# A mixer kernel: background steps drawn twice per merge-gate chunk, transposes of p in steps of their own, the last RG-LRU inputs cut earlier, copies of q and k ahead of their squares

## The chip, the cores and the metric

The kernel runs on one core of one Trainium2 chip. The metric is the device time of one execution in microseconds (us). A core has TensorE (PE, matmuls and transposes), VectorE (DVE), ScalarE (ACT), GpSimd (POOL) and SyncE (SP, which here issues the loads of weights). Each takes its own instructions in the order written for it and waits on semaphores for the others.

## What is computed

One layer of an encoder on 512 tokens of width 1024, in float32:

```python
x = x + FFN_RES * _swiglu(_rmsnorm(x, norm_ffn1[l]), w_ffn1_gu[l], w_ffn1_down[l])
...
h = _rmsnorm(x, norm_mix[l])
xr, gr, q, k, v, ga, gb = jnp.split(h @ w_in[l], splits, axis=-1)
xc = _centred_dwconv(xr, conv_w[l], conv_b[l]).astype(jnp.float32)
...
y_lru = ((h_fwd + h_bwd) * jax.nn.gelu(gr.astype(jnp.float32))).astype(x.dtype)
...
y_att = _neighbourhood_attention(q, k, v, rel_pos_bias[l]).astype(x.dtype)
y = jax.nn.sigmoid(ga) * y_lru + jax.nn.sigmoid(gb) * y_att
x = x + y @ w_out[l]
x = x + FFN_RES * _swiglu(_rmsnorm(x, norm_ffn2[l]), w_ffn2_gu[l], w_ffn2_down[l])
```

`h_fwd` and `h_bwd` are the recurrence `_rglru_scan` over `xc` forward and backward. It needs two sigmoid gates (a block-diagonal product with `xc`), an exponential, a square root and a scan over the tokens, in each direction. The attention has 16 heads of width 64; a query sees a window of 8 rows by 16 columns of the 8 x 64 token grid, with a learned bias and a softmax; `q` and `k` are normalized per head.

## The kernel before

**Precision and dense work.** A float32 product is made of three matmuls of a rounded high part and a low part: `wh` by `xh`, `wh` by `xl`, `wl` by `xh`. Weights come in chunks of 128 x 1024 values (512 KB) by a DMA of SP into `wraw` (three buffers); ACT (line 138), or DVE for every second chunk of the merge gates (line 140), casts to `wh`, and DVE subtracts to get `wl` (line 141), four buffers each. I call the matmuls that work on such chunks *dense*; they read 512 columns and fill an accumulator in PSUM.

**PSUM.** Two pools of four banks: `acc` for dense products (and for the second half of the scores in the second half of the heads), `aux` for everything else on PE: gate products of the RG-LRU, transposes, scores, PV.

**Stages.** First feed-forward; then the mixer; then the second feed-forward. The mixer's dense work, in its order:
- eight chunks for `xr` (`feat_chunk`, lines 165 to 167), each followed by the convolution;
- token groups (`tok_group`, lines 761 to 763) for q, k and v of the first eight heads (hf = 0), then of the other eight (hf = 1): four chunks each, 96 dense matmuls, into all four `acc` banks. The evictions at a group's end free the banks for the next group: the copies of q and k on ACT (line 774, each followed by a square at line 775), those of v on DVE (line 785);
- merge gates (`gates`, line 947): 24 chunks of 24 dense matmuls, eight for the GeLU gate, eight for each merge gate; each chunk is evicted on DVE to a `pair` tile (line 953);
- eight chunks of the output projection.

**Background.** Two generators hold the other work: lane "lru" (`lru`, line 642) and lane "att" (`heads`, line 806). `weave(rate)` is called after each chunk and draws from each lane as many steps as the table `RATE` gives for the phase ("xr", "t0" for the first half's q, k, v, "t1" for the second's, "g" for the gates); what a step issues then stands in the program behind that chunk. So the tables `LRU_PLAN` (which step of lane "lru" does what) and `RATE` (how many steps per chunk) set the order on all engines, apart from instructions marked `high_priority`, which a scheduler puts ahead of others on their engine where their inputs allow.

**Lane "lru".** For each of eight feature blocks f: `fetch` loads the gate weights; `cut` splits the convolved block into `ch` (ACT, line 138) and `cl` (DVE, line 141); `gates` does 12 groups of matmuls (line 675) and four sigmoids on ACT (line 685), and its next block waits for them; then `use`, `decay` (an exponential, line 705), `root` (a square root, line 710) and `scan` (DVE, lines 717 and 719, and an add at 720). Activations of a kind are kept together by `act`, since each change of kind needs a table load on ACT.

**Lane "att".** For each pair of heads fi of a half: `start` transposes q and k (lines 828 and 830) into two `aux` banks, which ACT and DVE empty into `qh`, `ql` (line 835), `kh`, `kl` (line 837); `scores` (line 854) makes the products, DVE adds the bias and takes the maximum (line 866, output `so` and `nmx`), ACT takes the exponential (869), DVE scales (875); `turn` transposes p (line 883) into an `aux` bank, copied to `PT` by ACT (886); `apply` multiplies with v (line 895, PV), copied to `att` by ACT (905). In the first half a unit is half a pair's keys (`n2` = 0 or 1), in the second a whole pair. One step holds the scores of unit i, PV of unit i - 2, the transposes of q and k for the next pair and the turns of unit i - 1; in the second half a yield lies between the turns of n2 = 0 and n2 = 1.

Of the kernel before, what the change touches and what calls it, by code (L numbers as in the profile page):

```python
# [11 lines left out]
AF = mybir.ActivationFunctionType  # L12
# [7 lines left out]
KT = D // P  # L20
# [37 lines left out]

LRU_PLAN = [
    ("root", range(4), range(39, 47)),  # L60
    ("scan", range(4), range(41, 49)),
    ("cut", range(8), (0, 3, 8, 13, 18, 23, 44, 48)),
    ("fetch", range(8), (0, 4, 9, 14, 19, 24, 44, 48)),
    ("gates", range(8), (2, 7, 12, 17, 22, 27, 47, 51)),
    ("decay", range(4), range(29, 37)),
# [8 lines left out]
]  # L74

RATE = {
    "xr": {"lru": 2.5, "att": 0.0},
    "t0": {"lru": 3, "att": 0.0},
    "t1": {"lru": 2, "att": 0.75},
    "g": {"lru": 3, "att": 0.85},  # L80
}


# [1 line left out]
def block_kernel(ctx: ExitStack, tc, a, out):  # L85
    nc = tc.nc
# [20 lines left out]
    def big_t(dt=F32, shape=(P, T), n="b"):  # L107
        return big.tile(list(shape), dt, tag="big", bufs=NBIG, name=nm(n))
# [55 lines left out]
    def mm3(ps, wh, wl, xh, xl, first, last, skip=False):  # L164
        nc.tensor.matmul(ps, wh, xh, start=first, stop=False, skip_group_check=skip)  # L165
        nc.tensor.matmul(ps, wh, xl, start=False, stop=False, skip_group_check=skip)  # L166
        mark["mm"] = nc.tensor.matmul(ps, wl, xh, start=False, stop=last, skip_group_check=skip)  # L167

    def feat_chunk(src, nk, xh, xl, ps, k0, ktot, act=True):
        H, L = load_w(src, nk * P, act)  # L170
        for k in range(nk):
            s = slice(k * P, (k + 1) * P)
            kk = k0 + k
            mm3(ps, H[:, s], L[:, s], xh[kk], xl[kk], kk == 0, kk == ktot - 1)


    def make_xg(gcol, tag):
# [350 lines left out]
    xh, xl, ssum, one, square = make_xg(C_G1, "a")  # L528
# [53 lines left out]
    xh, xl, ssum = nxt["v"][:3]  # L582
# [154 lines left out]
    for f in range(KT):  # L737
        ps = acc_t()
# [13 lines left out]
    def tok_group(w, hf):  # L752
        pss = [acc_t() for _ in range(NCB)]
        for kp in range(4):
            H, L = load_w(a["wqkv"][w * 2 + hf, kp], 1024)
            for j in range(NCB):
                tj = slice(j * P, (j + 1) * P)
                for k in range(2):
                    kk = kp * 2 + k
                    s = slice(k * T, (k + 1) * T)  # L760
                    nc.tensor.matmul(pss[j], xh[kk][:, tj], H[:, s], start=kk == 0, stop=False)  # L761
                    nc.tensor.matmul(pss[j], xl[kk][:, tj], H[:, s], start=False, stop=False)  # L762
                    mark["mm"] = nc.tensor.matmul(pss[j], xh[kk][:, tj], L[:, s], start=False, stop=kk == KT - 1)  # L763
            if kp < 3:
                weave(RATE[phase[0]])
        return pss

    def qk_raw(w, hf, st):
        raws = []
        for j, ps in enumerate(tok_group(w, hf)):  # L770
            t = big_t(n="qk")
            sq = big_t(n="sq")
            with tc.high_priority():
                nc.scalar.activation(t, ps, AF.Copy)
            nc.scalar.activation(sq, t, AF.Square)
            nc.vector.reduce_sum(st[:, w, j, :], sq.rearrange("p (h d) -> p h d", d=HD), axis=AX.X)
            raws.append(t)
        weave(RATE[phase[0]])
        return raws

# [25 lines left out]
    def heads(hf, raws, st):  # L806
# [9 lines left out]
        for w in range(2):  # L816
            for j in range(NCB):
                t = raws[w][j].rearrange("p (h d) -> p h d", d=HD)
# [95 lines left out]
        LB, LC = ATT_LAG[hf]  # L914
        for i in range(len(units) + LC):
            if i < len(units):
                fi, n2s = units[i]
                last = scores(fi, n2s)
                if i >= LC and 1 in units[i - LC][1]:
                    apply(units[i - LC][0], last)  # L920
                if 0 in n2s:
                    if fi < 3:
                        start(fi + 1)
                    if hf * 4 + fi + 1 < KT:
                        bias(hf * 4 + fi + 1)
            for n2 in (0, 1):
                if 0 <= i - LB < len(units) and n2 in units[i - LB][1]:
                    for hp in range(2):
                        turn(units[i - LB][0], n2, hp)
                if hf == 1 and n2 == 0:  # L930
                    yield
            if len(units) <= i < len(units) + LC and 1 in units[i - LC][1]:
                apply(units[i - LC][0])
            yield

    att = [None] * KT
# [10 lines left out]
    def gates(w, fs, fn, scale=1.0):  # L947
        q = [pair_t() for _ in range((len(fs) + 1) // 2)]
        for i, f in enumerate(fs):
            ps = acc_t()  # L950
            feat_chunk(a["wg3"][w * KT + f], KT, xh, xl, ps, 0, KT, f % 2 == 0)
            with tc.high_priority():
                nc.vector.tensor_tensor(q[i // 2][:, i % 2], ps, rb, ALU.mult)
            weave(RATE[phase[0]])
        for i, t in enumerate(q):
            n = min(2, len(fs) - 2 * i)
            nc.scalar.activation(t[:, :n], t[:, :n], fn, scale=scale)
        return [(f, q[i // 2][:, i % 2]) for i, f in enumerate(fs)]
# [126 lines left out]
```

## Time and profile before

| | |
|---|---|
| median of 3 runs | 1127.6 us (1127.58 to 1127.77) |
| the profiled execution | 1127.92 us |
| its span in the trace | 1125.7 us |
| busy: PE, DVE, ACT, POOL | 99%, 74%, 53%, 5% |
| mean granted clock of PE | 1.0 |

The span is the time from the first to the last instruction of the profiled execution; 2.2 us of its time lie outside it. A row of a timeline gives the start in us from the span's beginning, the duration, the engine, the line, the operation, the tiles it writes and reads, the shape, a count, and in brackets the idle time ahead of it with who ended it. Matmuls are pipelined: a row's duration is longer than the distance to the next start, and the distance is what counts. A list of waits adds up the idle time of an engine by the line that waited and the instruction that released it.

### The profile page before, as it was taken

How to read it: one execution, taken by the hardware profiler on the slowest of the kernel's cores; microseconds unless marked ns; L12 is line 12 of the kernel's file. 1: busy time of each engine (PE TensorE's matmuls, PEld its weight loads, DVE VectorE, ACT ScalarE, POOL GpSimd, SP SyncE). 2: the span in 40 equal slices, each digit the busy share in tenths (PEclk: the TensorE clock that was granted, in tenths of full speed). 3: DMA queues.
4: the chain of work that ended last, by engine and by line, in shares of the span. 5: the costliest groups of instructions: out<-in, count | busy, mean ns of one | idle time of the engine just before them, and what ended most of it. 6: DMA issues, size and time to landing. Idle time of an engine off the chain costs nothing.

```text
span 1125.7 us, 17414 instructions
## 1 busy us (share of the span) xinstructions
PE 1114.5 (99%) x6867; PEld 983.4 (87%) x6867; DVE 834.9 (74%) x1294; ACT 592.9 (53%) x897; POOL 52.3 (5%) x116
## 2 busy tenths in 40 slices
PE   9999999999999999999999999999999999999998
PEld 8899999988888777777888888888999999998887
DVE  7888888893736865899655877659688888894552
ACT  8554554563533668687464445446445445464330
POOL 0000000000000341120110000000000000000000
PEclk9999999999999999999999999999999999999999
DMA  7242333443423686573443342355134233252421
GB/s 265 93 127 80 114 112 95 132 134 98 143 80 103 164 231 174 151 193 94 135 147 103 94 124 64 105 180 183 57 95 118 90 112 114 94 169 94 131 75 38
DMA packets 46770, 138.04 MB, mean 123 GB/s; under 512 B 7008, under 2 KB 10592, under 8 KB 46688
## 3 DMA queue, kind: packets, MB, share of 16 engines
q1 hardware_dynamic: 39744, 118.31, 33.8%
q0 software_dynamic: 6368, 18.36, 5.9%
q8 instruction: 54, 0.88, 0.3%
q10 hardware_dynamic: 576, 0.26, 0.1%
q14 instruction: 28, 0.23, 0.1%
HBM read 120.12 MB, written 8.39 MB: 114 GB/s over the span
## 4 chain that ended last, share of the span: by engine, by line
PE 96%; DVE 2%; issue 1%; ACT 1%; DVEq 0%; ACTq 0%
PE acc L289 29%; PE acc L165 11%; PE acc L166 11%; PE acc L167 11%; PE aux L289 5%; PE aux L167 4%; PE aux L165 4%; PE aux L166 4%; PE acc L761 3%; PE acc L763 3%; PE acc L762 3%; PE aux L883 1%; PE aux L895 1%; PE aux L675 1%; PE aux L854 1%
## 5 line engine op out<-in xcount | busy, mean ns | idle before, releaser
L138 ACT ACTIVATE wh<-wraw 128x1024 fp32r<-128x1024 f32 (+3 forms) x242 | 239.8, 993 | 327.5 <-PE acc L289 95.9
L141 DVE TENSOR_TENSOR wl<-wraw,wh 128x1024 fp32r<-128x1024 f32 (+3 forms) x254 | 289.5, 1142 | 143.4 <-ACT wh L138 140.1
L289 PE MATMUL acc<-s,wh 128*128 128x256 f32 x1216 | 220.5, 283 | 0.0
L289 PEld LDWEIGHTS acc<-s,wh 128*128 128x128 f32 x1216 | 189.7, 192 | 0.0
L289 PE MATMUL acc<-s,wl 128*128 128x256 f32 x608 | 172.1, 283 | 0.0
L165 PE MATMUL acc<-xh,wh 128*128 128x512 f32 x304 | 120.4, 396 | 0.0
L167 PE MATMUL acc<-xh,wl 128*128 128x512 f32 x304 | 118.9, 391 | 0.0
L166 PE MATMUL acc<-xl,wh 128*128 128x512 f32 x304 | 118.8, 391 | 0.0
L289 PEld LDWEIGHTS acc<-s,wl 128*128 128x128 f32 x608 | 116.8, 192 | 0.0
L289 PE MATMUL acc<-xh,wl 128*128 128x256 f32 x304 | 86.0, 283 | 0.0
L289 PE MATMUL acc<-xl,wh 128*128 128x256 f32 x304 | 86.0, 283 | 0.0
L289 PE MATMUL acc<-xh,wh 128*128 128x256 f32 x304 | 86.0, 283 | 0.0
L761 PE MATMUL acc<-wh,xh 128*128 128x512 f32 x192 | 75.8, 396 | 1.9 <-DVE v L785 1.4
L762 PE MATMUL acc<-wh,xl 128*128 128x512 f32 x192 | 75.1, 391 | 0.0
L763 PE MATMUL acc<-wl,xh 128*128 128x512 f32 x192 | 75.0, 391 | 0.0
L323 DVE TENSOR_TENSOR wraw<-wraw,pair 128x1024 f32<-128x1024 f32 x57 | 69.5, 1220 | 0.8
L165 PE MATMUL aux<-hh,wh 128*128 128x512 f32 (+1 forms) x181 | 69.9, 386 | 0.0
L166 PE MATMUL aux<-hl,wh 128*128 128x512 f32 (+1 forms) x181 | 69.9, 386 | 0.0
L167 PE MATMUL aux<-hh,wl 128*128 128x512 f32 (+1 forms) x181 | 69.9, 386 | 0.0
L167 PE MATMUL acc<-hh,wl 128*128 128x512 f32 (+1 forms) x176 | 67.9, 386 | 0.0
L166 PE MATMUL acc<-hl,wh 128*128 128x512 f32 (+1 forms) x176 | 67.9, 386 | 0.0
L165 PE MATMUL acc<-hh,wh 128*128 128x512 f32 (+1 forms) x176 | 67.9, 386 | 0.0
(212 smaller groups left out, 2206.8 us busy)
## 6 DMA issues: line engine op xcount, KB each, us to landing
wraw<-wqkv SPq DMA_DIRECT2D x24, 512.0 KB, 4.5
wraw<-wg SPq DMA_DIRECT2D x24, 512.0 KB, 3.6
wraw<-w1d SPq DMA_DIRECT2D x22, 512.0 KB, 3.6
wraw<-w2d SPq DMA_DIRECT2D x22, 512.0 KB, 3.6
pair<-w2s SPq DMA_DIRECT2D x20, 512.0 KB, 3.6
wraw<-w2s SPq DMA_DIRECT2D x20, 512.0 KB, 3.6
wraw<-w1s SPq DMA_DIRECT2D x18, 512.0 KB, 3.6
pair<-w1s SPq DMA_DIRECT2D x18, 512.0 KB, 3.7
```

Of the source, the lines that this page charges most:

```text
L138: nc.scalar.activation(H, raw, AF.Copy)
L141: nc.vector.tensor_tensor(L, raw, H.bitcast(F32), ALU.subtract)
L165: nc.tensor.matmul(ps, wh, xh, start=first, stop=False, skip_group_check=skip)
L166: nc.tensor.matmul(ps, wh, xl, start=False, stop=False, skip_group_check=skip)
L167: mark["mm"] = nc.tensor.matmul(ps, wl, xh, start=False, stop=last, skip_group_check=skip)
L289: nc.tensor.matmul(o, w_[:, c], x_, start=first and m + k == 0 and w_ is H and x_ is xh_, stop=m + k == 4 and w_ is L, skip_group_check=True)
L323: nc.vector.tensor_tensor(t, t, o, ALU.add)
L675: prev, mm = mm, nc.tensor.matmul(ps[d][b], W[w][o, c], X[x][o], start=x == 1, stop=w + x == 0)
L761: nc.tensor.matmul(pss[j], xh[kk][:, tj], H[:, s], start=kk == 0, stop=False)
L762: nc.tensor.matmul(pss[j], xl[kk][:, tj], H[:, s], start=False, stop=False)
L763: mark["mm"] = nc.tensor.matmul(pss[j], xh[kk][:, tj], L[:, s], start=False, stop=kk == KT - 1)
L854: mm = hold(nc.tensor.matmul(ps[hp][:, i * 256 : (i + 1) * 256], q_[o, n * P : (n + 1) * P], keys(k_[o]), start=k_ is kl, stop=q_ is ql))
```

## The change

Five edits, in two tables and three functions:

- `LRU_PLAN`: the last two cuts (f = 6 and 7) move from steps 44 and 48 to steps 41 and 45; the scans of f = 0 to 3 move from steps 41..48 to 42, 43, 44, 46..50.
- `RATE`: lane "lru" runs at 2.75 instead of 2.5 steps per chunk in "xr" and 3.25 instead of 3 in "t0". In the gates the rates become 1.5 and 0.7, and `feat_chunk` draws once in the middle of each chunk as well as `gates` at its end, so 3 and 1.4 steps per chunk where they were 3 and 0.85.
- `qk_raw`: all four copies of a group are issued first, then the four squares, each behind the last copy.
- `heads`: in the gates a yield lies between a unit's scores and the turns of the unit before, and the turns of n2 = 0 and of n2 = 1 are steps of their own in both halves.
- `gates` passes the rate to `feat_chunk` for the draw in the middle.

```diff
--- before.py
+++ after.py
@@ -58,8 +58,8 @@
 
 LRU_PLAN = [
...
-    ("scan", range(4), range(41, 49)),
-    ("cut", range(8), (0, 3, 8, 13, 18, 23, 44, 48)),
+    ("scan", range(4), (42, 43, 44, 46, 47, 48, 49, 50)),
+    ("cut", range(8), (0, 3, 8, 13, 18, 23, 41, 45)),
...
@@ -74,10 +74,10 @@
 ]
 
 RATE = {
-    "xr": {"lru": 2.5, "att": 0.0},
-    "t0": {"lru": 3, "att": 0.0},
+    "xr": {"lru": 2.75, "att": 0.0},
+    "t0": {"lru": 3.25, "att": 0.0},
...
-    "g": {"lru": 3, "att": 0.85},
+    "g": {"lru": 1.5, "att": 0.7},
 }
 
 
@@ -166,12 +166,14 @@
         nc.tensor.matmul(ps, wh, xl, start=False, stop=False, skip_group_check=skip)
         mark["mm"] = nc.tensor.matmul(ps, wl, xh, start=False, stop=last, skip_group_check=skip)
 
-    def feat_chunk(src, nk, xh, xl, ps, k0, ktot, act=True):
+    def feat_chunk(src, nk, xh, xl, ps, k0, ktot, act=True, mid=None):
         H, L = load_w(src, nk * P, act)
         for k in range(nk):
             s = slice(k * P, (k + 1) * P)
             kk = k0 + k
             mm3(ps, H[:, s], L[:, s], xh[kk], xl[kk], kk == 0, kk == ktot - 1)
+            if mid is not None and k == nk // 2 - 1:
+                weave(mid)
 
 
     def make_xg(gcol, tag):
@@ -767,14 +769,15 @@
 
     def qk_raw(w, hf, st):
         raws = []
-        for j, ps in enumerate(tok_group(w, hf)):
+        for ps in tok_group(w, hf):
             t = big_t(n="qk")
+            with tc.high_priority():
+                copy = nc.scalar.activation(t, ps, AF.Copy)
+            raws.append(t)
+        for j, t in enumerate(raws):
             sq = big_t(n="sq")
-            with tc.high_priority():
-                nc.scalar.activation(t, ps, AF.Copy)
-            nc.scalar.activation(sq, t, AF.Square)
+            after(nc.scalar.activation(sq, t, AF.Square), copy)
             nc.vector.reduce_sum(st[:, w, j, :], sq.rearrange("p (h d) -> p h d", d=HD), axis=AX.X)
-            raws.append(t)
         weave(RATE[phase[0]])
         return raws
 
@@ -923,12 +926,14 @@
                         start(fi + 1)
                     if hf * 4 + fi + 1 < KT:
                         bias(hf * 4 + fi + 1)
-            for n2 in (0, 1):
-                if 0 <= i - LB < len(units) and n2 in units[i - LB][1]:
+            if phase[0] == "g":
+                yield
+            if 0 <= i - LB < len(units):
+                for k, n2 in enumerate(units[i - LB][1]):
+                    if k:
+                        yield
                     for hp in range(2):
                         turn(units[i - LB][0], n2, hp)
-                if hf == 1 and n2 == 0:
-                    yield
             if len(units) <= i < len(units) + LC and 1 in units[i - LC][1]:
                 apply(units[i - LC][0])
             yield
@@ -948,7 +953,7 @@
         q = [pair_t() for _ in range((len(fs) + 1) // 2)]
         for i, f in enumerate(fs):
             ps = acc_t()
-            feat_chunk(a["wg3"][w * KT + f], KT, xh, xl, ps, 0, KT, f % 2 == 0)
+            feat_chunk(a["wg3"][w * KT + f], KT, xh, xl, ps, 0, KT, f % 2 == 0, RATE[phase[0]])
             with tc.high_priority():
                 nc.vector.tensor_tensor(q[i // 2][:, i % 2], ps, rb, ALU.mult)
             weave(RATE[phase[0]])
```

PE, DVE and ACT have the same number of instructions before and after, and POOL and SP the same DMAs. Where they stand is shown at three places.

DVE from the last scans to the eviction of v of the first half (`wl` are low parts of weights; `cl` is the low part of block 7, the last one cut, which the last gate products wait for; `th<-gate,gate` are scans, `v<-acc` the evictions). Before:

```order
L720 TENSOR_TENSOR th_730_4291<-th_730_4291,th_736_4328 128x512
L717 SCALAR_TENSOR_TENSOR th_753_4401<-gate_698_4186,gate_699_4187 128x512
L719 SCALAR_TENSOR_TENSOR th_754_4404<-gate_701_4195,gate_702_4196 128x512
L141 TENSOR_TENSOR wl_854_4901<-wraw_852_4899,wh_853_4900 128x1024
L720 TENSOR_TENSOR th_753_4401<-th_753_4401,th_754_4404 128x512
L141 TENSOR_TENSOR wl_857_4939<-wraw_855_4937,wh_856_4938 128x1024
L141 TENSOR_TENSOR cl_820_4765<-xc_692_4162,ch_819_4764 128x512
L141 TENSOR_TENSOR wl_863_4989<-wraw_861_4987,wh_862_4988 128x1024
L785 TENSOR_SCALAR v_840_4870<-acc_794_4642,rcol_594_3718 128x512
L785 TENSOR_SCALAR v_841_4872<-acc_795_4643,rcol_594_3718 128x512
L785 TENSOR_SCALAR v_842_4874<-acc_796_4644,rcol_594_3718 128x512
L785 TENSOR_SCALAR v_843_4876<-acc_797_4645,rcol_594_3718 128x512
```

and after, from the cut of block 7 on, whose `cl` is the second row:

```order
L713 TENSOR_TENSOR gate_693_4147<-gate_693_4147,th_750_4371 128x512
L141 TENSOR_TENSOR cl_800_4657<-xc_706_4206,ch_799_4656 128x512
L713 TENSOR_TENSOR gate_696_4156<-gate_696_4156,th_754_4404 128x512
L722 TENSOR_TENSOR th_697_4162<-th_697_4162,th_700_4169 128x512
L719 SCALAR_TENSOR_TENSOR th_730_4291<-gate_663_4016,gate_664_4017 128x512
L721 SCALAR_TENSOR_TENSOR th_733_4298<-gate_666_4025,gate_667_4026 128x512
L141 TENSOR_TENSOR wl_839_4852<-wraw_837_4850,wh_838_4851 128x1024
L722 TENSOR_TENSOR th_730_4291<-th_730_4291,th_733_4298 128x512
L719 SCALAR_TENSOR_TENSOR th_750_4371<-gate_692_4146,gate_693_4147 128x512
L721 SCALAR_TENSOR_TENSOR th_754_4404<-gate_695_4155,gate_696_4156 128x512
L722 TENSOR_TENSOR th_750_4371<-th_750_4371,th_754_4404 128x512
L141 TENSOR_TENSOR wl_856_4921<-wraw_854_4919,wh_855_4920 128x1024
```

The last cl stood behind the scans and two wl; it now stands ahead of two pairs of scans and their adds, and the evictions of v begin behind five more rows, with no cl among them.

ACT at the end of the group for k of the second half (`qh`, `kh` are the high parts of one pair of heads, `qk<-acc` the copies that free the accumulators, `sq` the squares, `wh` a cast of weights). Before:

```order
L834 ACTIVATE qh_907_5260<-aux_905_5250,gq8_3677 128x4x128
L138 ACTIVATE wh_985_5606<-wraw_984_5605 128x1024
L836 ACTIVATE kh_909_5262<-aux_906_5251,small_78 128x512
L774 ACTIVATE qk_916_5302<-acc_877_5088 128x512
L775 ACTIVATE sq_917_5303<-qk_916_5302 128x512
L774 ACTIVATE qk_918_5307<-acc_878_5089 128x512
L775 ACTIVATE sq_919_5308<-qk_918_5307 128x512
L774 ACTIVATE qk_920_5312<-acc_879_5090 128x512
L775 ACTIVATE sq_921_5313<-qk_920_5312 128x512
L774 ACTIVATE qk_922_5317<-acc_880_5091 128x512
L775 ACTIVATE sq_923_5318<-qk_922_5317 128x512
```

and after:

```order
L837 ACTIVATE qh_907_5263<-aux_905_5253,gq8_3677 128x4x128
L839 ACTIVATE kh_909_5265<-aux_906_5254,small_78 128x512
L775 ACTIVATE qk_916_5305<-acc_877_5101 128x512
L775 ACTIVATE qk_917_5307<-acc_878_5102 128x512
L138 ACTIVATE wh_985_5606<-wraw_984_5605 128x1024
L775 ACTIVATE qk_918_5309<-acc_879_5103 128x512
L775 ACTIVATE qk_919_5311<-acc_880_5104 128x512
L779 ACTIVATE sq_920_5313<-qk_916_5305 128x512
L779 ACTIVATE sq_921_5316<-qk_917_5307 128x512
L779 ACTIVATE sq_922_5319<-qk_918_5309 128x512
L779 ACTIVATE sq_923_5322<-qk_919_5311 128x512
```

The cast of weights stood ahead of kh and of all copies and now stands behind kh and two copies; the squares, which alternated with the copies, follow all four.

PE in the merge gates around the transposes of p (`ident,p`) of one pair of heads (`ident,qk` are the transposes of the next pair's q and k, `acc<-xh,wh` and its like dense matmuls). Before, behind the third scores of the second half and a PV:

```order
L830 MATMUL aux_1235_6866<-ident_83,qk_916_5302 128x8x16
L830 MATMUL aux_1235_6866<-ident_83,qk_918_5307 128x8x16
L830 MATMUL aux_1235_6866<-ident_83,qk_920_5312 128x8x16
L830 MATMUL aux_1235_6866<-ident_83,qk_922_5317 128x8x16
L883 MATMUL aux_1242_6887<-ident_83,p_1177_6615 128x128 x4
L165 MATMUL acc_1246_6901<-xh_482_3088,wh_1248_6903 128x512
L166 MATMUL acc_1246_6901<-xl_483_3089,wh_1248_6903 128x512
L883 MATMUL aux_1244_6894<-ident_83,p_1180_6625 128x128 x4
L167 MATMUL acc_1246_6901<-xh_482_3088,wl_1249_6904 128x512
```

and after:

```order
L165 MATMUL acc_1232_6815<-xh_488_3094,wh_1234_6817 128x512
L166 MATMUL acc_1232_6815<-xl_489_3095,wh_1234_6817 128x512
L167 MATMUL acc_1232_6815<-xh_488_3094,wl_1235_6818 128x512
L886 MATMUL aux_1236_6834<-ident_83,p_1169_6538 128x128 x4
L886 MATMUL aux_1238_6841<-ident_83,p_1172_6548 128x128 x4
L165 MATMUL acc_1232_6815<-xh_490_3096,wh_1234_6817 128x512
L166 MATMUL acc_1232_6815<-xl_491_3097,wh_1234_6817 128x512
L167 MATMUL acc_1232_6815<-xh_490_3096,wl_1235_6818 128x512
```

The eight transposes of p stood behind the transposes of q and k, four and four with two dense matmuls between them; they now stand in the middle of a chunk, with dense matmuls on both sides, half a chunk or more behind the scores.

## The prediction

> **What bounds the kernel now.** I read the page's busy times first, then the list of TensorE's (PE's) waits, then the timeline of PE, VectorE (DVE) and ScalarE (ACT) around each wait. The page's first line and the whole list of waits (engine, line waited at, who released it; total us, times, longest):
>
> ```profile
> PE 1114.5 (99%) x6867; PEld 983.4 (87%) x6867; DVE 834.9 (74%) x1294; ACT 592.9 (53%) x897; POOL 52.3 (5%) x116
> PE aux L675 <- DVE cl L141: 1.4, 2, 1.2
> PE acc L761 <- DVE v L785: 1.4, 1, 1.4
> PE aux L883 <- ACT att L905: 1.2, 1, 1.2
> PE aux L131 <- DVE pol L600: 1.1, 1, 1.1
> PE aux L289 <- ACT wh L138: 0.9, 1, 0.9
> PE aux L883 <- DVE nmx L866: 0.7, 2, 0.4
> PE aux L883 <- DVE kl L837: 0.6, 1, 0.6
> PE acc L761 <- ACT qk L774: 0.5, 1, 0.5
> ```
>
> PE is busy for 99% of the span, so the time is PE's work plus these waits, 7.8 us in all. The change moves instructions and removes none (the order holds 6615 rows on PE before and after, and as many on DVE and ACT), so PE's work stays and only waits can come or go. Two rows lie in stages that the change doesn't touch: pol (1.1) at the start and wh at L289 (0.9) in the first feed-forward. That leaves 5.8 us that the change can reach, in the token groups and the merge gates, plus what a wait costs beyond its idle time. Two of the waits on PE (start, duration, line, idle before):
>
> ```profile
> 473.28 0.39 PE L761 MATMUL acc<-wh,xh 128*128 128x512 f32 x1
> 474.87 0.50 PE L675 MATMUL aux<-cl,wh 64*128 64x512 f32 x2 [1.20 <-DVE cl L141]
> ...
> 478.65 0.39 PE L762 MATMUL acc<-wh,xl 128*128 128x512 f32 x1
> 478.88 0.39 PE L763 MATMUL acc<-wl,xh 128*128 128x512 f32 x1
> 480.64 0.50 PE L761 MATMUL acc<-wh,xh 128*128 128x512 f32 x1 [1.38 <-DVE v L785]
> ```
>
> A dense matmul follows the last by 0.23 us (478.65 to 478.88). Over the first wait the starts lie 1.59 apart: 0.23 is due, 1.20 is idle, 0.16 is refilling the pipeline. Over the second: 1.76 - 0.23 - 1.38 = 0.15. So each wait costs its idle time and 0.16.
>
> **The change part by part.** *The cut of the last gate blocks earlier (plan steps 41 and 45 for 44 and 48), scans later.* Why PE waited at 474.87 and 480.64, on DVE and on ACT:
>
> ```profile
> 473.00 1.22 DVE L141 TENSOR_TENSOR wl<-wraw,wh 128x1024 fp32r<-128x1024 f32 x1
> 474.13 0.68 DVE L141 TENSOR_TENSOR cl<-xc,ch 128x512 fp32r<-128x512 f32 x1
> 478.70 1.23 DVE L141 TENSOR_TENSOR wl<-wraw,wh 128x1024 fp32r<-128x1024 f32 x1 [3.89 <-ACT wh L138]
> 479.85 2.71 DVE L785 TENSOR_SCALAR v<-acc,rcol 128x512 f32<-128x512 f32 x4
> ```
>
> ```profile
> 475.88 1.84 ACT L685 ACTIVATE pair<-aux,small 128x512 f32<-128x512 f32 x3 [3.76 <-PE aux L675]
> 477.61 1.07 ACT L138 ACTIVATE wh<-wraw 128x1024 fp32r<-128x1024 f32 x1
> ...
> 479.27 1.28 ACT L705 ACT_TABLE_LOAD   x1
> 480.56 0.72 ACT L705 ACTIVATE gate<-gate,sn 128x512 f32<-128x512 f32 x1
> ```
>
> The last cl stood behind the scans and a weight's wl, and landed 0.06 us before PE started at 474.87. The late gate block made the sigmoids late (475.88), these the weight cast (477.61), this the wl (478.70), and behind it on DVE stood the eviction of v that frees PE's accumulator. So it is one lateness, paid twice. After the change both cl stand ahead of the scans they stood behind, and the last gate block lies 48 dense matmuls ahead of the end of the v group, where it lay 11 ahead. Both cl waits (1.4) go. The v wait goes if the longer chain fits: how long the sigmoids of the gate block before took after its last matmul, on PE and on ACT:
>
> ```profile
> 464.65 0.39 PE L675 MATMUL aux<-ch,wh 64*128 64x512 f32 x2
> ```
>
> ```profile
> 466.91 1.83 ACT L685 ACTIVATE pair<-aux,small 128x512 f32<-128x512 f32 x3
> ```
>
> The sigmoids ended at 468.74, 3.7 us after the block's end at 465.04. Behind them ACT now has a table load (1.29 to the next start), three exponentials (3 x 0.72) and a weight cast (1.07), then DVE a wl (1.15 to the next start) and the eviction (0.79 from its start at 479.85 to PE's at 480.64): 3.7 + 1.3 + 2.2 + 1.1 + 1.15 + 0.8 = 10.2 us, against 48 x 0.23 = 11.0. It fits by 0.8 us, so I count the 1.4 as gone, and keep 1.4 for the range.
>
> In this trace a table load holds ACT for 1.28 us and the next activation starts 1.29 after it. The Trainium skill ("ScalarE: Activation LUTs", section What ACT_TABLE_LOAD costs) adds a drain of about 1.38 us to every switch. By that price the chain would be about 11.6 us and 0.6 us of the v wait would stay; the rows at 479.27 and 480.56 leave no room for such a drain, so I don't take it.
>
> *Copies of q and k first; scans ahead of ql and kl.* The next token-group end, DVE and then ACT:
>
> ```profile
> 527.03 0.75 DVE L835 SCALAR_TENSOR_TENSOR ql<-aux,gq,qh 128x512 fp32r<-128x512 f32 x1
> 527.69 1.22 DVE L717 TENSOR_TENSOR_SCAN th<-gate,gate 128x512 f32<-128x512 f32 x1
> 528.82 1.20 DVE L141 TENSOR_TENSOR wl<-wraw,wh 128x1024 fp32r<-128x1024 f32 x1
> 529.94 0.75 DVE L837 SCALAR_TENSOR_TENSOR kl<-aux,small,kh 128x512 fp32r<-128x512 f32 x1
> ```
>
> ```profile
> 528.86 0.59 ACT L774 ACTIVATE qk<-acc 128x512 f32<-128x512 f32 x1
> ```
>
> PE waited for the first copy (0.5; it frees an accumulator) and for kl (0.6; it frees the aux buffer of the second transposes of p). A cast of weights stood ahead of the copy on ACT, a scan and a wl ahead of kl on DVE. In the changed order kh and two copies come ahead of that cast, and kl stands directly behind ql: both waits go, 1.1. The squares are later by at most three copies (under 2 us), and nothing on PE reads them before the next heads. The price: the scans now stand ahead of the first head's ql and kl, for which the first scores wait, and these now come 24 dense matmuls behind their transposes instead of 28. This place is tight by my reading; I take nothing for it, and one scan and a wl (1.2 + 1.2 less the cover) gives at most 1 us for the range.
>
> *Transposes of p in steps of their own.* PE and ACT at the two waits in the merge gates:
>
> ```profile
> 660.91 0.38 PE L854 MATMUL aux<-kl,qh 64*128 64x256 f32 x2
> ...
> 663.05 0.60 PE L830 MATMUL aux<-ident,qk 128*128 128x128 f32 x4
> 663.90 0.66 PE L883 MATMUL aux<-ident,p 128*128 128x128 f32 x4 [0.25 <-DVE nmx L866]
> ...
> 682.13 0.40 PE L166 MATMUL acc<-xl,wh 128*128 128x512 f32 x1
> 683.75 0.66 PE L883 MATMUL aux<-ident,p 128*128 128x128 f32 x4 [1.22 <-ACT att L905]
> ```
>
> ```profile
> 683.12 0.57 ACT L905 ACTIVATE att<-aux 128x512 f32<-128x512 f32 x1
> ```
>
> In both, transposes of p ask for an aux buffer directly behind scores, PV or the transposes of q and k, which hold the four there are. In the changed order no transposes of p in the gates stand behind scores: at least 12 dense matmuls (2.8 us) lie between. The att copy that came 1.2 late has then the time it needs, and nmx too: 1.2 + 0.3 (0.7 in the list less the 0.4 below) go. The other nmx wait, at the transposes behind the second q and k of the first half, keeps its place in both orders: 0.4 stays. The same matmuls stand in about as many pieces between dense ones, so PE gains or loses nothing by the cutting itself.
>
> *What is new at the end.* The last PV moves from the last gates chunk's end to two and a half chunks earlier; it had covered PE while the last chunk was evicted and combined. DVE there:
>
> ```profile
> 732.40 0.69 DVE L953 TENSOR_TENSOR pair<-acc,rstd 128x512 f32<-128x512 f32 x1 [2.17 <-PE acc L167]
> ...
> 734.93 0.69 DVE L975 SCALAR_TENSOR_TENSOR pair<-pair,att 128x512 f32<-128x512 f32 x1 [0.45 <-ACT att L905]
> ...
> 737.11 0.69 DVE L141 TENSOR_TENSOR yl<-pair,yh 128x512 fp32r<-128x512 f32 x1 [0.76 <-ACT yh L138]
> ```
>
> The chain ends at 737.80; without the wait for att (0.45) at 737.35, 4.95 us after the eviction's start. PE comes to that yl after 22 dense matmuls of the output projection, 22 x 0.23 = 5.06. It just fits; I take 0.1 us, 0.5 for the range.
>
> **Sum.** Gone: 1.4 + 1.4 + 0.5 + 0.6 + 1.2 + 0.3 = 5.4 us idle in seven waits, and 7 x 0.16 = 1.1 of refilling: 6.5. New: 0.1. The profiled execution took 1127.9 us (span 1125.7 and 2.2 around it), so 1121.5; against the median of 1127.6, which is 0.3 less, 1121.2.
>
> **The rivals.**
> 1. *The lateness of the LRU lane only shifts (0.17).* DVE and ACT do the same work; if the v eviction stays late (1.4 + 0.16) and kl at the first scores costs some 0.5, 2.1 us come back: 1123.3. For it: the fits of 0.8 and less. Against: at 480 us DVE had idled 3.89 before the wl, so it has room.
> 2. *The aux buffers only change hands in the merge gates (0.12).* Score steps come 36 and 48 dense matmuls apart instead of 72 and 48; the 1.5 there and its refilling (0.3) come back at other instructions: 1123.0. Both rivals together: 1125.1.
> 3. *Slower: DVE falls behind in the gates (0.04).* One score step on DVE, first and last rows:
>
> ```profile
> 663.07 0.42 DVE L866 CUSTOM_DVE_ANT_0 so<-aux,bm 128x256 f32<-128x256 f32 x1
> ...
> 669.43 0.61 DVE L875 TENSOR_SCALAR p<-p,rs 128x256 f32<-128x256 f32 x2
> ```
>
> That is 7.0 us, and a gates chunk needs about 2.6 more (eviction 0.69, wl 1.22, one combine 0.69). Between the first two score steps, 36 matmuls apart, PE takes 36 x 0.23 + 2.7 (660.91 to 663.65) = 11.0 us, and DVE needs 7.0 + 1.5 x 2.6 = 10.9: full. Scores hold two of four accumulators; if a chunk's eviction comes to stand behind a whole softmax, PE waits from the point at which that is later than the next chunk's 5.5 us: 7.0 - 5.5 = 1.5 a chunk. At both chunks of all four steps that is 12 us: 1133. Against: the steps after the second are 48 apart with 16 transposes and a PV besides, and the evictions have priority.
> 4. *It does not do what it says (0.08).* Each wait is replaced by one of the same size, because what is late is the weights' arrival: 1127.6. Against: no row of PE's list names a DMA.
>
> **How the numbers follow.** My forecast has 0.59, at 1121.2. The low end is all reachable waits gone with the 0.4 that I left and a larger price of refilling: 1127.6 - 7.4 = 1120.2; the high end takes rivals 1 and 2, near 1125. About 0.2% (2.3 us) is what a measurement of this kernel can tell from no change; faster by more means below 1125.3. Forecast, 1 and 2 are faster: 0.88, less 0.01 for both together going over; no change 0.09; slower 0.04.
>
> **What would show it.** PE's list of waits after should hold pol 1.1, wh L289 0.9, one nmx of 0.4 and little else; cl, v, att, kl and qk gone, and PE's busy time within 1 us of 1114.5. A v or kl row of over 0.5 near 480 and 520 us is rival 1, aux rows after 630 us rival 2, acc waits for the pair's eviction in the gates rival 3. I am wrong if the span shortens by less than 4 us, or if PE's busy time is what moved.

## The result, and the profile after

The changed kernel takes 1122.05 us (median of 5, 1121.8 to 1122.5) against 1127.69 us (5 runs) for the kernel before: 5.6 us less, ratio 0.995 with a 95% interval of 0.9936 to 0.9963. The forecast was 1121.2, in a range of 1120.2 to 1125.0. The profiled execution took 1122.16 us with a span of 1119.9, 5.8 less than before. Line numbers differ a little from kernel to kernel, since the edits add lines: the scores, line 854 before, are line 857 here. PE's whole list of waits is now:

```profile
PE aux L131 <- DVE pol L602: 1.1, 1, 1.1
PE aux L291 <- ACT wh L138: 0.9, 1, 0.9
PE aux L857 <- DVE kl L840: 0.9, 1, 0.9
PE aux L886 <- DVE nmx L869: 0.4, 1, 0.4
```

The first line of the page has:

```profile
PE 1113.1 (99%) x6867; PEld 983.9 (88%) x6867; DVE 835.1 (75%) x1294; ACT 593.0 (53%) x897; POOL 52.4 (5%) x116
```

PE has as many instructions as before and is busy for 1.4 us less than the 1114.5 before, which is more than the 1 us that the prediction allowed. That is not less work: refilling counts as busy (the row behind the wait at 480.64 lasts 0.50 us, the next one 0.39), and the prediction had 1.1 us of it going. The other 4.4 us of the 5.8 are time in which PE was idle: span less busy time was 11.2 and is 6.8.

cl, v, att, qk, the kl wait at the transposes of p and one of the two nmx are gone. The two waits at other stages and the other nmx stayed. One row is new: PE's scores (line 857) waited 0.9 for the first kl (line 840). PE, and DVE ahead of that kl:

```profile
516.03 0.39 PE L765 MATMUL acc<-wl,xh 128*128 128x512 f32 x1
517.31 0.39 PE L857 MATMUL aux<-kl,qh 64*128 64x256 f32 x2 [0.90 <-DVE kl L840]
```

```profile
509.05 1.22 DVE L719 TENSOR_TENSOR_SCAN th<-gate,gate 128x512 f32<-128x512 f32 x1
510.18 1.20 DVE L721 TENSOR_TENSOR_SCAN th<-gate,gate 128x512 f32<-128x512 f32 x1
511.30 1.20 DVE L719 TENSOR_TENSOR_SCAN th<-gate,gate 128x512 f32<-128x512 f32 x1
512.41 0.67 DVE L722 TENSOR_TENSOR th<-th,th 128x512 f32<-128x512 f32 x1
513.00 1.22 DVE L721 TENSOR_TENSOR_SCAN th<-gate,gate 128x512 f32<-128x512 f32 x1
514.13 1.20 DVE L141 TENSOR_TENSOR wl<-wraw,wh 128x1024 fp32r<-128x1024 f32 x1
515.25 0.69 DVE L722 TENSOR_TENSOR th<-th,th 128x512 f32<-128x512 f32 x1
515.85 0.75 DVE L838 SCALAR_TENSOR_TENSOR ql<-aux,gq,qh 128x512 fp32r<-128x512 f32 x1
516.51 0.75 DVE L840 SCALAR_TENSOR_TENSOR kl<-aux,small,kh 128x512 fp32r<-128x512 f32 x1
```

Read the brackets: none of the DVE rows has one. DVE ran without a pause and had four scans, two adds and a wl to do before ql. kl ended at 517.26, PE had been free for it at 516.26. By starts it costs PE 1.28 - 0.23 = 1.05 us.

At the end of the v group, where PE had waited 1.4, the eviction now starts at 474.43, and PE asks for that bank near 477.2 (48 dense matmuls behind the last gate block's end):

```profile
473.29 1.23 DVE L141 TENSOR_TENSOR wl<-wraw,wh 128x1024 fp32r<-128x1024 f32 x1 [0.26 <-ACT wh L138]
474.43 1.40 DVE L788 TENSOR_SCALAR v<-acc,rcol 128x512 f32<-128x512 f32 x2
```

The last place the prediction had called just fitting is the output projection's first need of the last yl. PE's starts there lie 0.36 and 0.34 apart instead of 0.23, so it costs 0.13 and 0.11 of refilling: 0.24 us.

```profile
733.03 0.39 PE L165 MATMUL acc<-yh,wh 128*128 128x512 f32 x1
733.39 0.50 PE L166 MATMUL acc<-yl,wh 128*128 128x512 f32 x1
733.73 0.39 PE L167 MATMUL acc<-yh,wl 128*128 128x512 f32 x1
```

### The profile page after: what moved, and what is told of

Same layout as the page of the kernel before. It is cut to its first block, busy times and chain, and to the rows that moved or that the text cites. A ratio compares the mean times of both kernels' runs of the same rounds, so it can differ in the third digit from the quotient of the medians.

```text
span 1119.9 us, 17423 instructions
## 1 busy us (share of the span) xinstructions
PE 1113.1 (99%) x6867; PEld 983.9 (88%) x6867; DVE 835.1 (75%) x1294; ACT 593.0 (53%) x897; POOL 52.4 (5%) x116
## 4 chain that ended last, share of the span: by engine, by line
PE 99%; DVE 0%; ACT 0%; issue 0%; ACTq 0%; DVEq 0%
PE acc L291 29%; PE acc L165 11%; PE acc L166 11%; PE acc L167 11%; PE aux L291 5%; PE acc L763 4%; PE acc L765 4%; PE acc L764 4%; PE aux L165 4%; PE aux L166 4%; PE aux L167 4%; PE aux L898 1%; PE aux L886 1%; PE aux L677 1%; PE aux L857 1%; PE acc L404 1%
## 5 line engine op out<-in xcount | busy, mean ns | idle before, releaser
L165 PEld LDWEIGHTS acc<-xh,wh 128*128 128x128 f32 x304 | 57.1, 188 | 12.8 <-issue 1.7
```

## The experiments

Each kernel's time stands beside the kernel before on the same chip, which took 1128.09 us beside the first four, 1127.79 beside the next four and 1127.87 beside the last four; what is compared is the difference from it.

| run | us | against before |
|---|---|---|
| lru_only | 1123.81 | -4.28 |
| plan_only | 1124.81 | -3.28 |
| copies_only | 1128.19 | +0.10 |
| attention_only | 1126.43 | -1.66 |
| after_again | 1122.09 | -5.70 |
| kl_ahead | 1120.99 | -6.80 |
| copies_back | 1121.89 | -5.90 |
| cut_back | 1125.39 | -2.40 |
| no_mid_draw | 1126.61 | -1.26 |
| pace_double | 1134.66 | +6.79 |
| kl_ahead_copies_back | 1121.81 | -6.06 |
| kl_ahead_nmx | 1120.64 | -7.23 |

### The parts alone, on the kernel before

**lru_only**: the tables of the RG-LRU lane.

```diff
-    ("scan", range(4), range(41, 49)),
-    ("cut", range(8), (0, 3, 8, 13, 18, 23, 44, 48)),
+    ("scan", range(4), (42, 43, 44, 46, 47, 48, 49, 50)),
+    ("cut", range(8), (0, 3, 8, 13, 18, 23, 41, 45)),
...
-    "xr": {"lru": 2.5, "att": 0.0},
-    "t0": {"lru": 3, "att": 0.0},
+    "xr": {"lru": 2.75, "att": 0.0},
+    "t0": {"lru": 3.25, "att": 0.0},
```

> The kernel before with only the two tables of the RG-LRU lane changed (plan, rates in xr and t0). Theory: each wait has its own cause in the order. Both cl waits (1.4), the v wait (1.4) and the kl wait at the second transposes (0.6) go, with 0.16 of refilling each: 4.0; the new kl wait at the first scores (0.9 and 0.16) comes with these tables, because the scans now stand ahead of ql and kl: 1127.7 - 4.0 + 1.1 = 1124.8. The qk wait (0.5), nmx and att stay as they were. Rival: the new kl wait belongs to the attention edit; then it is absent here and the time is 1123.7.

Measured 4.28 us under the kernel before (ratio 0.9964, interval 0.995 to 0.9978), 1.4 us more than the theory's 2.9. The cl, v and kl waits are gone, and so is the qk wait near 529, which I had not expected of these tables. A qk wait of 0.4 has come up at another place, and kl at the first scores is short. From the timeline of PE:

```profile
502.12 0.39 PE L762 MATMUL acc<-wh,xl 128*128 128x512 f32 x1
502.90 0.50 PE L761 MATMUL acc<-wh,xh 128*128 128x512 f32 x1 [0.40 <-ACT qk L774]
...
516.96 0.39 PE L763 MATMUL acc<-wl,xh 128*128 128x512 f32 x1
517.45 0.39 PE L854 MATMUL aux<-kl,qh 64*128 64x256 f32 x2
```

Both waits here belong to one thing: kl ended at 517.39 by DVE's own pace; PE, held back 0.55 at 502, came that much later and waited that much less. So the new kl wait does come with these tables, and most of it was hidden behind another wait. By its number the rival (4.0 under, no kl row) was nearer than the theory; its reason falls with copies_back below, which has the attention edit and no kl row either.

**plan_only**: the first two pairs of lines above, without the rates.

> The kernel before with only the plan's cuts and scans changed; the last gate block then stands 24 dense matmuls ahead of the v group's end, where it stood 11 ahead before and 48 after. As the prediction put it, the v wait is the cl's lateness paid a second time: both go, 2.8 and 0.5 of refilling, 1124.4. Rival: the v wait hangs on how far ahead the block stands, not on when cl landed: behind the block come sigmoids, a weight cast and a wl, 2.5 to 3.7 + 1.1 + 1.15 + 0.8 = 5.5 to 6.7 us, against 24 x 0.23 = 5.5; 0 to 1.2 us of v stays, 1124.4 to 1125.6, and the kl and qk rows stay.

Measured 3.28 under (0.9961 to 0.9983), which is the first theory's 3.3. No cl and no v row is left; kl and qk stand as before:

```profile
PE aux L883 <- DVE kl L837: 0.6, 1, 0.6
PE acc L761 <- ACT qk L774: 0.5, 1, 0.5
```

More than half of the change's gain is in these two lines of the plan. 24 dense matmuls between the last gate block and the end of the group are enough. This run can't tell the theory from its rival, which allowed for 0 to 1.2 us of v; cut_back below does.

**copies_only**: the copies ahead of the squares.

```diff
-        for j, ps in enumerate(tok_group(w, hf)):
+        for ps in tok_group(w, hf):
             t = big_t(n="qk")
-            sq = big_t(n="sq")
             with tc.high_priority():
-                nc.scalar.activation(t, ps, AF.Copy)
-            nc.scalar.activation(sq, t, AF.Square)
+                copy = nc.scalar.activation(t, ps, AF.Copy)
+            raws.append(t)
+        for j, t in enumerate(raws):
+            sq = big_t(n="sq")
+            after(nc.scalar.activation(sq, t, AF.Square), copy)
             nc.vector.reduce_sum(st[:, w, j, :], sq.rearrange("p (h d) -> p h d", d=HD), axis=AX.X)
-            raws.append(t)
```

> The kernel before with only the copies of q and k ahead of the squares. By the sum of the prediction the qk wait goes, 0.5 and 0.16: 1127.0. Rival: the kl wait stands 0.3 us behind it on PE and ends at a fixed time on DVE (kl lands at 530.7 whatever PE does before), so it grows by what the first one gives up, or more, since the cast of weights now comes later and the wl and kl stand behind it on DVE: kl 1.2 to 2.2 and a time of 1127.7 to 1128.5.

Measured no difference (ratio 1.0001, 0.9991 to 1.001). But neither theory had it: the qk wait did not go, so nothing could move to kl. ACT at that place:

```profile
527.57 1.06 ACT L138 ACTIVATE wh<-wraw 128x1024 fp32r<-128x1024 f32 x1 [0.49 <-PE acc L762]
528.53 0.67 ACT L837 ACTIVATE kh<-aux,small 128x512 fp32r<-128x512 f32 x1
529.10 2.05 ACT L773 ACTIVATE qk<-acc 128x512 f32<-128x512 f32 x4
```

PE waits for the first copy, and ahead of the first copy stands no square in either order, but the cast and kh. The edit puts three squares behind copies that PE waits for less. It does bring something elsewhere, and loses it again. Near 432 and 505 us, at the copies of other groups, PE's starts lay up to 0.34 apart before, delays too short for the list of waits, and there this kernel gains 0.4 to 0.5. But its cl row has grown from 1.4:

```profile
PE aux L675 <- DVE cl L141: 2.1, 2, 1.3
```

The first of the two cl ends at 463.60 on DVE (463.33 before), and PE, which came earlier, only waits longer for it.

**attention_only**: the yields, the draw in the middle of a gates chunk and the rates of the gates, as in the diff of the change.

> The kernel before with only the attention edit: turns in steps of their own, draws in the middle of a gates chunk, the gates' rates. Theory: one nmx wait (0.3, refilled twice) and att (1.2) go, by the distances of starts 0.7 + 1.4 = 2.1: 1125.6; cl, v, kl at the second transposes and qk stay. Rival 2 of the prediction: the aux buffers only change hands in the gates, other aux rows of the same size appear after 600 us, 1127.

Measured 1.66 under (0.9977 to 0.9996, so 0.5 to 2.6). The trace has no att row and one nmx of 0.4, and cl, v, kl and qk as before. No aux row is new in the gates, so rival 2 falls. A 0.4 at line 404, at the kernel's start, is in this profile and not in that of before; this edit doesn't reach there.

```profile
PE aux L885 <- DVE nmx L868: 0.4, 1, 0.4
PE aux L404 <- DVE wh L389: 0.4, 1, 0.4
```

That row does not account for the difference of 2.1 and 1.66. The gates alone, from their first dense matmul to the first of the output projection, take 172.35 us before (561.84 to 734.19) and 170.68 here (561.91 to 732.59), 1.67 less. What is missing is the price of the cutting. In that stretch PE goes from dense matmuls to small ones and back 19 times before and 25 times here. Without its two waits the stretch before would be 170.25, and here it is 170.68 with the same matmuls and no wait: 0.43 for six more pieces, 0.07 each. The way back to dense matmuls shows it, with 0.31 between the first two starts and 0.23 or 0.24 from then on:

```profile
584.40 1.03 PE L885 MATMUL aux<-ident,p 128*128 128x128 f32 x8
585.19 0.48 PE L165 MATMUL acc<-xh,wh 128*128 128x512 f32 x1
585.50 0.40 PE L166 MATMUL acc<-xl,wh 128*128 128x512 f32 x1
585.74 0.39 PE L167 MATMUL acc<-xh,wl 128*128 128x512 f32 x1
```

The parts add up to -4.28 + 0.10 - 1.66 = -5.84, the whole measured -5.64 and -5.70: in sum they hardly act on each other, though one pair does (below).

### The new wait, and the changed kernel with one part undone

**after_again**: the changed kernel, unchanged.

> The changed kernel once more, beside the others on their chip: 5.6 us under the kernel before, with the kl wait of 0.9 at the first scores.

5.70 under, with the kl wait of 0.9.

**kl_ahead**: three of the four scans of blocks 6 and 7 later.

```diff
-    ("scan", range(6, 8), range(68, 72)),
+    ("scan", range(6, 8), (68, 72, 73, 74)),
```

> The changed kernel with the second scan of block 6 and both scans of block 7 moved from steps 69 to 71 to steps 72 to 74, so that ql and kl of the first heads stand ahead of two scans (2.4 us) and an add on DVE. Theory: the new wait is DVE's backlog standing ahead of kl; it goes whole, 0.9 and 0.16, and nothing takes its place: 1.06 under the changed kernel. Rival: the backlog only moves on to the next scores' maximum and the second transposes of p, which wait for DVE too; then a wait of about 0.5 to 1 appears near 524 us and the gain is under 0.5.

Measured 1120.99, 1.10 under the changed kernel on the same chip, and the theory had 1.06. (Of the four executions of each, the longest here took 1121.53 and the shortest there 1122.00.) kl now ends at 514.0, ahead of PE, and two scans follow it:

```profile
513.26 0.74 DVE L840 SCALAR_TENSOR_TENSOR kl<-aux,small,kh 128x512 fp32r<-128x512 f32 x1
513.92 1.22 DVE L719 TENSOR_TENSOR_SCAN th<-gate,gate 128x512 f32<-128x512 f32 x1
515.05 1.20 DVE L721 TENSOR_TENSOR_SCAN th<-gate,gate 128x512 f32<-128x512 f32 x1
```

DVE does the same work before and after; two scans that nobody waits for were ahead of one subtraction that PE waits for. No wait appears behind it, so the rival falls.

**copies_back**: the change without its edit of the copies (the diff of copies_only, reversed).

> The changed kernel with copies and squares of q and k alternating as before. Theory from the runs of the parts: the copies' edit brings nothing by itself; the qk wait of 0.4 (with refilling 0.56) near 502 us comes back, and the kl wait near 517, which ends at a time that DVE sets, shrinks from 0.9 to about 0.1: 0.2 under the changed kernel or the same. By the prediction's sum the edit is worth 0.66, and this kernel is 0.66 over the changed one.

Measured 1121.89, 0.20 under the changed kernel, as the theory had it and not 0.66 over; the difference itself lies within the intervals. The list has the qk row, and no kl row:

```profile
PE acc L763 <- ACT qk L776: 0.4, 1, 0.4
```

**kl_ahead_copies_back**: both of these edits.

> kl_ahead with copies and squares alternating as before. With DVE's backlog out of the way nothing hides the first copy's lateness: the qk wait of 0.4 near 502 us costs its 0.56 in full, 0.5 to 0.6 over kl_ahead. If the copies' edit is worth nothing in any order, no difference.

Measured 6.06 under the kernel before where kl_ahead is 6.80 under: 0.74 over it, expected 0.5 to 0.6, and the list has the same qk row of 0.4. The two ran on different chips and 0.74 lies within the intervals, but the traces agree: from the first dense matmul of the token groups to the first of the gates PE takes 152.65 us here and 151.86 in kl_ahead, 0.79 less. So the edit of the copies is worth nothing where PE waits for kl behind it (152.83 in the changed kernel, 152.85 in copies_back), and 0.7 to 0.8 where that wait is gone.

**cut_back**: the change with the last two cuts at their old steps.

```diff
-    ("cut", range(8), (0, 3, 8, 13, 18, 23, 41, 45)),
+    ("cut", range(8), (0, 3, 8, 13, 18, 23, 44, 48)),
```

> The changed kernel with only the last two cuts put back to steps 44 and 48. The last gate block then stands 35 dense matmuls ahead of the v group's end, with its cl behind scans again. Theory: a cl wait comes back (about 1 us), and the v wait does not, since 35 x 0.23 = 8.0 us hold the sigmoids, a cast, a wl and the eviction (5.5 to 6.7): about 1.2 over the changed kernel. Rival: any late cl is paid twice; then v comes back too and the kernel is 2.5 or more over.

Measured 3.3 over the changed kernel, where the theory had 1.2 and the rival 2.5 or more. The rival's number fits, its reason doesn't; PE's list shows that neither mechanism is the whole:

```profile
PE aux L677 <- DVE cl L141: 1.3, 1, 1.3
PE aux L857 <- DVE kl L840: 1.2, 1, 1.2
...
PE aux L833 <- DVE qk L822: 1.0, 4, 0.3
```

The cl wait comes back and the v wait does not, as the theory had it: v hangs on how far the block stands ahead of the group's end. But with the late block other work of the lane stands ahead on DVE, and the normalization of k (line 822; its last rows start at 510.88, and at 502.00 in the changed kernel) is late for the transposes of k: four waits of 0.37 to 0.49 by their starts, 1.85 in all. 1.43 for cl, 1.85 for these and 0.3 for a longer kl are 3.6, near the 3.3.

### The pace in the gates

**no_mid_draw**: the change without the draw in the middle of a chunk.

```diff
-            feat_chunk(a["wg3"][w * KT + f], KT, xh, xl, ps, 0, KT, f % 2 == 0, RATE[phase[0]])
+            feat_chunk(a["wg3"][w * KT + f], KT, xh, xl, ps, 0, KT, f % 2 == 0)
...
-    "g": {"lru": 1.5, "att": 0.7},
+    "g": {"lru": 3, "att": 1.4},
```

> The changed kernel without the draw in the middle of a gates chunk: 3 and 1.4 steps at each chunk's end, the yields as in the change. Transposes of p then stand directly behind scores or q and k transposes at two places of the second half (16 of them at a chunk's end at another two). If the cure is the distance from the scores, a part of the two waits (nmx 0.25, att 1.2) comes back, 0.5 to 1.5 us over the changed kernel; if the yields alone are the cure, it stays within 0.2.

Measured 4.4 over the changed kernel (1124.91 to 1127.86). That is outside both of the expected ranges. Of the two waits only nmx came back (0.25); the loss is elsewhere. At the first scores of the second half two steps are drawn at once, and the scores stand directly behind the transposes of q and k that they need:

```profile
631.73 0.60 PE L833 MATMUL aux<-ident,qk 128*128 128x128 f32 x4
635.00 0.58 PE L857 MATMUL aux<-kl,qh 64*128 64x256 f32 x2 [2.67 <-DVE kl L840]
635.38 0.42 PE L857 MATMUL aux<-kh,qh 64*128 64x256 f32 x2
```

So the yields alone don't do: without the draw in the middle the rate of 1.4 puts two dependent steps side by side. This wait costs 2.83 by its starts and nmx 0.42. PE's clock was halved for 3.41 us behind it (last section), which by an estimate from that length costs half of it, 1.7; and the gates are cut into 19 pieces again, which saves the 0.43 from above. Together 4.5, near the 4.4.

**pace_double**: `"g": {"lru": 1.5, "att": 1.5}` instead of 0.7 in the change.

> The changed kernel with lane att drawn at 1.5 instead of 0.7 per half chunk in the gates, so that the score steps of the second half stand 24 dense matmuls apart. Rival 3 of the prediction: from about 36 apart DVE has more to do between two score steps (7.0 and 2.6 a chunk) than PE leaves time for; at 24 apart PE takes 24 x 0.23 + 2.7 + 1.8 to 3.9 = 10 to 12 us and DVE 9.6, with squares, combines and adds of the RG-LRU besides: waits of PE for DVE of 1 to 2 us at each of three steps, 3 to 6 us over the changed kernel. If DVE's queue doesn't decide, within 1 us.

Measured 1134.66, 6.8 over the kernel before and 12.5 over the changed one, on the same measure. The direction is rival 3's, but most of its price is not: the largest rows are dependent steps drawn together, not the softmax.

```profile
PE aux L831 <- DVE qk L822: 3.6, 4, 2.9
PE aux L857 <- DVE kl L840: 2.5, 2, 1.6
PE aux L886 <- DVE nmx L869: 1.2, 2, 0.8
```

Of the waits at the score steps themselves there are nmx with 1.00, PT with 0.54 and att with 0.64 by their starts: 2.2 us. PE's clock was halved here too, for 6.83 us (last section), 3.4 by the same estimate as above. No row says that an accumulator waited for a pair's eviction, which was rival 3's mechanism.

**kl_ahead_nmx**: kl_ahead with a yield ahead of the turns of the third unit of the first half too (and of the second, where it stands already).

```diff
-            if phase[0] == "g":
+            if phase[0] == "g" or i == 2:
                 yield
```

> kl_ahead with one more yield, between the third scores of the first half and the transposes of p behind them, so that these stand a chunk later instead of behind the second pair's q and k. Theory: the last nmx wait (0.4, by the distance of starts 0.66) goes: 0.6 under kl_ahead, about 1120.4 where the kernel before has 1127.7. Rival: the steps behind it shift by a chunk and the last PV and output chain meet (qk transposes cut into three, two applies of PV near the end), and a new wait eats the gain.

Measured 1120.64, 7.23 under the kernel before (0.9918 to 0.9951) where kl_ahead is 6.80 under; expected 0.6 more, found 0.4. That difference too lies within the intervals; the traces have 0.48, from the first dense matmul of the token groups to the first of the output projection (322.53 us in kl_ahead, 322.05 here). The whole list of waits of PE is what lies outside the mixer:

```profile
PE aux L131 <- DVE pol L602: 1.1, 1, 1.1
PE aux L291 <- ACT wh L138: 0.9, 1, 0.9
```

It has the shortest time of the kernels here.

## Why the prediction was right

**Right, with the mechanism.** PE's work stayed and only waits went; seven waits and their refilling were to go, 6.5 us, and all seven went. By distances of starts they had cost 6.7 (the nmx place was refilled twice, 0.7 instead of 0.46). The cl and v waits went with the plan alone, 3.28 of a predicted 3.3. The attention part brought 1.66 of 2.1. The output chain cost 0.24 where I took 0.1. The table load's chain ahead of the v eviction, which I had at 10.2 of 11.0 us, left about 2 us to spare (474.43 + 0.79 against 477.2): the sigmoids ended 2.7 us behind the block instead of 3.7. The wait that the drain of the Trainium skill ("ScalarE: Activation LUTs", section What ACT_TABLE_LOAD costs) would have left there is not in the list; with 2 us to spare, 1.38 more would not have shown either, but the activation behind the load again starts 1.29 after it, on ACT of the changed kernel:

```profile
469.06 1.28 ACT L707 ACT_TABLE_LOAD   x1
470.35 1.96 ACT L707 ACTIVATE gate<-gate,sn 128x512 f32<-128x512 f32 x3
```

**The term that was mis-sized.** "This place is tight by my reading; I take nothing for it": the scans ahead of the first ql and kl. They cost 0.9 and the refilling, 1.05 to 1.06, at the upper end that I had kept (1 us). kl_ahead took the term away and brought 1.10. What should have been added up is DVE's queue: four scans, two adds, a wl, ql and kl are 8.2 us without a pause (509.05 to 517.26), and they begin less than a us before PE transposes q and k (509.92), while PE with these transposes and 24 dense matmuls is ready for the scores after 6.3 (516.26).

**A step that was wrong.** "The same matmuls stand in about as many pieces between dense ones, so PE gains or loses nothing by the cutting itself." In the gates there are 25 pieces where there were 19, and by attention_only they cost 0.43.

**How near the number was.** 6.7 gone, 1.05 for kl, 0.24 for the output chain and 0.43 for the pieces come: 5.0, and 5.64 was measured. Most of the rest are the short delays at the copies of q and k near 432 and 505 us, which I had not counted: they went as well, 0.4 to 0.5 in all. So of the terms that I had not counted or too small, some made the kernel slower, by 1.6, and some faster, by 0.6 to 0.7. That the forecast was off by only 0.9 is partly luck; that the seven waits would go was not.

**The step that was wrong though its number was right.** "In the changed order kh and two copies come ahead of that cast, and kl stands directly behind ql: both waits go, 1.1." They went, but not by the copies' edit: copies_only left both, and lru_only removed both. With the new tables alone kh (522.42) and the first copy (522.99) stand ahead of the cast (524.75) on ACT, where the cast came first before; why the order turned there was not tested. What the copies' edit removed is a third wait, at 502, that the new tables bring (0.4, in lru_only and copies_back), and its time was lost again in the kl wait until that was removed.

**"One lateness, paid twice"** held in the form that plan_only tested: both went together. cut_back shows what ties them. The late cl does not itself make v late; it makes the last gate block stand late in the order, and v waits when the block stands 11 dense matmuls ahead of the group's end, and not at 24, 35 or 48.

**The rivals.** 1 came in part: the lane's lateness did shift to kl, for 1.05 and not 2.1. 2 did not come. 3 did not come at the change's pace: two score steps started on DVE 10.5 us apart, with DVE busy for 10.2 of them, full as I had worked out (10.9), and PE did not wait.

```profile
634.65 0.42 DVE L869 CUSTOM_DVE_ANT_0 so<-aux,bm 128x256 f32<-128x256 f32 x1
...
645.16 0.42 DVE L869 CUSTOM_DVE_ANT_0 so<-aux,bm 128x256 f32<-128x256 f32 x1
```

At twice the pace it came from another side. 4 did not come.

## What to carry to other kernels

When an engine is busy for 99% and the same work is only reordered, add up its waits by the distance of starts, and then count for each moved piece what now stands ahead of the next thing the busy engine needs, on the engine that makes it: a "just fits" there is a term with a price, not a zero. Two waits in a row that end on the same engine are not two gains; removing the first may only lengthen the second, and an edit that looks worthless beside such a wait can be worth its full size once that is gone. Try the parts alone: here two lines of a table held more than half of the gain. And count the pieces: each time the small matmuls are cut once more between dense ones, PE pays a little (0.07 us here).

## What the runs showed of the hardware

A wait of PE can cost more than its length. In no_mid_draw PE was idle for 2.67 us, from 632.33 to 635.00, behind the last dense matmul (631.06) and eight transposes, and the granted clock in the windows around it (stretch, length and busy us with count, granted clock, DMA share, GB/s) halved:

```profile
632.00:634.40 2.40, 0.33 (x4) 1.00 0.00 0
634.40:637.60 3.20, 2.60 (x24) 0.50 0.55 164
637.60:642.00 4.40, 4.40 (x27) 0.97 0.27 89
```

The clock fell at 634.43, 2.1 us into the idle time, and came back at 637.84, so for 3.41 us PE had half of it: the score matmuls behind the wait start 0.21 apart (635.38 to 635.59) instead of 0.12. Waits of 0.9 to 1.4 us, as in the kernel before and the changed one, show nothing of the kind: the granted clock is 1.00 in the stretches that hold them. In pace_double the clock was at 0.50 from 604.35 to 611.18, for 6.83 us, in a stretch in which PE had first idled 2.9 and then worked in short pieces. The Trainium skill ("TensorE: Matmul & The Clock Gate", section Part 1: The HAM clock gate) has the clock fall after an idle window of about 3.4 us. The length agrees with the half-clock stretches here, 3.41 us and twice 3.41. But the idle time that was enough here is shorter than that: in the 3.41 us ahead of the fall PE still worked until 632.33. Whether transposes count as work there no run here shows.

The wide scatter of no_mid_draw goes with the clock. Four of its ten executions took 1124.9 to 1125.3 us at a mean granted clock of 0.999 to 1.000, six took 1126.6 to 1127.9 at 0.997 to 0.998; the profiled one is of the six. The gap of 1.9 us between the middles of the two groups is near the 1.7 that half a clock for 3.41 us costs by the estimate above. That the clock did not fall in the four is not shown by a trace, since only the profiled one has one.
